# Attention in a hybrid decoder layer: bias rows broadcast by TensorE out of SBUF, and part of the last head pair's weights transposed by TensorE

## Chip, cores and metric

The kernel runs on one core of a Trainium2 chip. The metric is the device time of one execution in microseconds (us), taken as the median of several runs. The five engines of the core that matter here are TensorE (PE, with its weight loads shown apart as PEld), VectorE (DVE), ScalarE (ACT), GpSimd (POOL) and SyncE (SP), whose queue issues most of the DMAs.

## What is computed

One layer of a decoder with two parallel head groups, over 2048 tokens of width 1024. The part that the change touches is the attention group with forget gates: 8 heads of width 64, causal, with a logit bias that is a running sum of log forget gates.

```python
def fox_attention(q, k, v, f_pre):
    log_f = jax.nn.log_sigmoid(f_pre.astype(jnp.float32))
    c = jnp.cumsum(log_f, axis=1).transpose(0, 2, 1)
    ...
        s = jnp.einsum('bhqd,bhkd->bhqk', qi, kh).astype(jnp.float32) * scale
        s = s + ci[..., :, None] - c[:, :, None, :]
        s = jnp.where(kpos[None, :] <= qpos[:, None], s, -jnp.inf)
        pr = jax.nn.softmax(s, axis=-1).astype(vh.dtype)
        return jnp.einsum('bhqk,bhkd->bhqd', pr, vh)
```

The query's own `ci` is the same for a whole row and drops out of the softmax, so the kernel only needs `c` of the keys: one row of 2048 numbers per head, the same for all 128 queries of a block. Around it stand an input projection, a chunkwise mLSTM group, an output projection, a squared-ReLU MLP, a gated embedding and three norms.

## The kernel before, in words

**Stages.** The mLSTM group comes first (up to about 540 us), then the attention, then output projection, MLP, gate and final norm. Attention works on four pairs of heads, j = 0 to 3 (`fox_attn`, called in a loop over `NP`), and inside a pair on two heads, `hh`. While a pair is attended to, a *filler* supplies TensorE with other work: the projections of the next pair (`fox_z`, tiles zfq, zv, zfk) and the embedding (`ple_parts`, tile pp), or, in the last pair, half of the output projection (`wo_parts`, tile om, line 641).

**A head.** The 16 blocks of 128 queries are taken in nine steps (`ROWS`): block 15 alone, then the pairs (14, 0), (13, 1) up to (8, 6), then block 7 alone. A step has 16 blocks of 128x128 weights (the last has 8), held in two *units* of 8 blocks. For each step `fox_rows` does:

- lines 798 to 803: score matmuls into PSUM tiles s (a pool of `SB` = 3) in chunks of up to 512 keys;
- line 806: DVE adds the bias row and takes the running maximum, into an SBUF tile sp;
- line 821: ACT takes the exponential, with the maximum as its bias;
- lines 826 and 828: ACT casts a unit to f16 (tile ph, `PHB` = 4 buffers), and POOL or DVE writes the rest as a second f16 part beside it;
- line 830: one DMA transpose on SP's queue turns the unit's 16 blocks (8 high, 8 low) into tile pt (`PTB` = 3 buffers).

`fox_av` (lines 846 to 849) multiplies a step's transposed weights by the values. It runs `LAG` = 3 steps behind the scores: a finished step goes into `avq`, and `drain` takes out the oldest.

**The bias.** In the gates stage `cf`, the running sums of all heads, is transposed on TensorE into `crs` [128 x 128], one row for each head and key block (line 376). Line 379 writes it to DRAM as `crow`. At the start of each head, lines 890 to 893 fetch it in two halves (`sg` = 1, then 0) of 1024 keys: SP's queue issues a DMA that reads 8 rows of `crow` into all 128 partitions (512 KB), and DVE multiplies the tile by the score scale. `bias` has two buffers, so that a half can only be fetched when the head before has added that half for the last time, and the first step of a head needs half 0 first.

**What sets the order.** The program is written in this order, and a scheduler then gives each engine a fixed sequence of instructions; an engine works through its own in order, and a queue of SP issues in order.

## Time and profile before

| | us |
|---|---|
| median of 3 runs (2952.34 to 2958.37) | 2958.08 |
| the profiled execution | 2954.44 |
| its span in the trace | 2952.7 |
| PE busy (share of the span) | 2698.4 (91%) |
| DVE busy | 1621.7 (55%) |
| ACT busy | 1008.3 (34%) |
| POOL busy | 698.7 (24%) |

The profile is of one execution, so its terms are set against its own time of 2954.44 us, of which 2952.7 us are the span. Busy time is the union of an engine's instructions. The shares are means over stages of different kinds: in the MLP, which is more than half of the span, PE is busy nearly without a break.

### The profile page before, as it was taken

How to read it: one execution, taken by the hardware profiler on the slowest of the kernel's cores; microseconds unless marked ns; L12 is line 12 of the kernel's file. 1: busy time of each engine (PE TensorE's matmuls, PEld its weight loads, DVE VectorE, ACT ScalarE, POOL GpSimd, SP SyncE). 2: the span in 40 equal slices, each digit the busy share in tenths (PEclk: the TensorE clock that was granted, in tenths of full speed). 3: DMA queues.
4: the chain of work that ended last, by engine and by line, in shares of the span. 5: the costliest groups of instructions: out<-in, count | busy, mean ns of one | idle time of the engine just before them, and what ended most of it. 6: DMA issues, size and time to landing. Idle time of an engine off the chain costs nothing. (4 is left out here: it accounts for less than half of the span.)

```text
span 2952.7 us, 45034 instructions
## 1 busy us (share of the span) xinstructions
PE 2698.4 (91%) x18229; PEld 1507.1 (51%) x18229; DVE 1621.7 (55%) x3633; ACT 1008.3 (34%) x1686; POOL 698.7 (24%) x435
## 2 busy tenths in 40 slices
PE   4998999888878788788999999999999999999997
PEld 2756767555454554343344444444444444444686
DVE  6464654766757657556654444444444444445636
ACT  6244444465555555553411111111111111113532
POOL 1011110244343444343122111111212111111132
PEclk9999999989899989999999999999999999999999
DMA  9212220387686879996700000000000000002623
GB/s 243 45 44 59 58 47 20 94 167 137 139 166 133 165 169 219 196 205 222 148 29 29 29 29 16 28 15 29 29 29 29 29 29 16 28 15 43 143 69 136
DMA packets 535265, 256.36 MB, mean 87 GB/s; under 512 B 432784, under 2 KB 502672, under 8 KB 535056
## 3 DMA queue, kind: packets, MB, share of 16 engines
q1 hardware_dynamic: 525296, 236.66, 35.0%
q10 hardware_dynamic: 9760, 16.82, 1.8%
q8 instruction: 142, 2.33, 0.3%
q14 instruction: 67, 0.55, 0.1%
HBM read 113.88 MB, written 32.60 MB: 50 GB/s over the span
## 5 line engine op out<-in xcount | busy, mean ns | idle before, releaser
L1054 PE MATMUL d<-wd_hl,hid 128*128 128x512 f16 x3072 | 678.2, 380 | 8.4 <-DVE x L1059 8.2
L1036 PE MATMUL h<-y1t,wu_hl 128*128 128x512 f16 x3072 | 673.5, 379 | 0.5 <-issue 0.5
L1054 PEld LDWEIGHTS <-hid 128*128 128x128 f16 x3072 | 301.3, 98 | 375.0 <-issue 15.8
L1036 PEld LDWEIGHTS <-wu_hl 128*128 128x128 f16 x3072 | 300.5, 98 | 363.2 <-ACT y1y L200 1.0
L1059 DVE SCALAR_TENSOR_TENSOR x<-d,fac,x 128x512 f32<-128x512 f32 x512 | 373.8, 747 | 132.2 <-PE d L1054 131.8
L1044 POOL TENSOR_TENSOR hid<-r,hid 128x512 f16<-128x512 f32 x128 | 174.5, 1364 | 765.2 <-ACT hid L1043 659.1
L1042 DVE SCALAR_TENSOR_TENSOR r<-h,r 128x512 f32<-128x512 f32 x128 | 88.3, 690 | 458.2 <-ACT r L1040 458.1
L1040 ACT ACTIVATE r<-h 128x512 f32<-128x512 f32 x128 | 75.9, 594 | 766.8 <-PE h L1036 763.3
L828 POOL TENSOR_TENSOR ph<-sp,ph 128x1024 f16<-128x1024 f32 x119 | 255.9, 2164 | 283.3 <-ACT ph L826 219.3
L271 PEld LDWEIGHTS <-yt 128*128 128x128 f16 x3072 | 251.6, 101 | 40.1 <-issue 13.7
L260 PE MATMUL zqk<-yt,wqk_hl 128*128 128x512 f16 x768 | 188.7, 393 | 27.9 <-DMA yt<-yy 27.9
L821 ACT ACTIVATE sp<-sp,nb,fs 128x1024 f32<-128x1024 f32 (+3 forms) x192 | 177.9, 982 | 85.2 <-DVE nb L818 60.5
L798 PE MATMUL s<-K,Q 128*128 128x512 f16 (+3 forms) x320 | 117.9, 369 | 79.4 <-DVE mx L806 76.4
L846 PE MATMUL av<-vt,pt 128*128 128x65 f16 x1088 | 121.9, 199 | 67.3 <-DMA pt<-ph 55.6
L271 PE MATMUL zvo<-wvo_hl,yt 128*128 128x256 f16 x1536 | 175.0, 275 | 4.1 <-ACT wvo_hl L155 2.8
L1007 PE MATMUL pg<-wpg_hl,y2t 128*128 128x256 f16 x1536 | 171.0, 275 | 4.7 <-DVE x L1059 4.0
L1007 PEld LDWEIGHTS <-y2t 128*128 128x128 f16 x1536 | 151.6, 99 | 24.1 <-issue 5.1
L826 ACT CAST ph<-sp 128x1024 f16<-128x1024 f32 x136 | 137.8, 1038 | 67.9 <-DMA pt<-ph 62.6
L846 PEld LDWEIGHTS <-pt 128*128 128x128 f16 x1088 | 105.3, 100 | 75.1 <-DMA pt<-ph 67.8
L806 DVE CUSTOM_DVE_ANT_0 sp<-s,bias,mx 128x512 f32<-128x512 f32 (+2 forms) x192 | 124.5, 648 | 29.4 <-POOL ph L828 14.2
L260 PEld LDWEIGHTS <-wqk_hl 128*128 128x128 f16 x768 | 77.4, 101 | 105.5 <-ACT wqk_hl L155 25.9
L641 PEld LDWEIGHTS <-mix 128*128 128x128 f16 x768 | 76.4, 102 | 101.6 <-issue 27.7
(380 smaller groups left out, 3648.2 us busy)
## 6 DMA issues: line engine op xcount, KB each, us to landing
x<-in_x_dram SPq DMA_DIRECT2D x32, 512.0 KB, 5.8
wu_st<-in_w_up_dram SPq DMA_DIRECT2D x16, 1024.0 KB
wd_st<-in_w_down_dram SPq DMA_DIRECT2D x16, 1024.0 KB, 4.9
bias<-crow SPq DMA_DIRECT2D x16, 512.0 KB, 5.9
pled<-fox_st ACTq DMA_DIRECT2D x32, 256.0 KB, 2.8
wod<-spare ACTq DMA_DIRECT2D x32, 256.0 KB, 5.0
wos<-wod SPq DMA_DIRECT2D x32, 256.0 KB, 3.9
emb<-pled SPq DMA_DIRECT2D x32, 256.0 KB, 3.0
```

What stands on the lines that cost most here:

```text
L260: PE.matmul(ps, lhsT=hl[:, a, kt, m * P:(m + 1) * P], rhs=yT[g][b][:, kt, :], start=i == 0, stop=i == 3 * KT - 1)
L271: PE.matmul(ps[:, 0:n], lhsT=yT[g][b][:, kt, o:o + P], rhs=hl[:, a, kt, 0:n], start=i == 0, stop=i == 3 * KT - 1)
L806: V.tensor_tensor_reduce(out=st[u][:, o * P:(o + n) * P], in0=ps[:, 0:n * P], in1=bias[kb // 8][:, kb % 8 * P:(kb % 8 + n) * P], scale=1.0 ...
L821: A.activation(sl_, sl_, AF.Exp, bias=nb, scale=fs[:, 0:1])
L826: A.copy(ph[:, 0:1024], st[u])
L828: eng.tensor_sub(ph[:, 1024:2048], st[u], ph[:, 0:1024])
L846: PE.matmul(ar, lhsT=pt[:, o, :], rhs=vs[:, 0:65], start=kb == 0, stop=False)
L1007: PE.matmul(ps, lhsT=aT[t // 4][ya][:, kt, o:o + P], rhs=hl[:, wa, kt, :], start=i == 0, stop=i == 3 * KT - 1)
L1036: PE.matmul(ps, lhsT=wu[:, a, kt, m * P:(m + 1) * P], rhs=y1T[g][b][:, kt, :], start=i == 0, stop=i == 3 * KT - 1)
L1044: T.tensor_sub(hid[:, 1, m], r2, hid[:, 0, m])
L1054: PE.matmul(ps, lhsT=hid[:, a, m, t * P:(t + 1) * P], rhs=wd[:, b, m, hf * 512:(hf + 1) * 512], start=i == 0, stop=i == 5)
L1059: V.scalar_tensor_tensor(xs, ps, fac, xs, ALU.mult, ALU.add)
```

## The change

It has two parts.

The first takes the bias broadcast off the DMA. `crs` becomes a constant tile that stays in SBUF, and `crow` and its DMA are gone. For each half of 1024 keys there are now two PSUM tiles of the score pool (`cb`, tag "s"). Each is filled by four f32 matmuls, whose stationary operand is one column of the identity repeated 128 times and whose moving operand is `crs`; each writes one row of `crs` to all 128 partitions. ACT then copies the tile to SBUF with the score scale as its factor, which replaces DVE's multiplication.

The second part concerns the last head pair alone (h of 6 and 7). Of the two units of a step, the second is no longer transposed by DMA: `fox_rows` puts it into `turns`, and `turn` transposes it when `drain` comes to it (one step ahead of its use): 16 transposing matmuls of 128x128 f16 into two PSUM tiles of the pool that the filler uses (tag "z"), and two ACT copies to pt. There are 8 such units in each of the two heads.

```diff
-    crow = dr.tile([P, P], F32, name="crow")
+    crs = const.tile([P, P], F32, name="crs")
+    identh = const.tile([P, P], F16, name="identh")
+    V.tensor_copy(identh, ident)
...
-        crs = gp.tile([P, P], F32, name="crs")
         V.tensor_copy(crs, tps[:, 0:P])
-        SP.dma_start(out=crow, in_=crs)
...
-            SP.dma_start_transpose(out=pt, in_=ph)
+            if h >= FH - 2 and u == 1:
+                turns[tag] = pt, ph
+            else:
+                SP.dma_start_transpose(out=pt, in_=ph)
             pts.append(pt)
         return pts
+
+    turns = {}
+
+    def turn(e):
+
+        tag = f"{e[3]}_{e[4][0]}" if e[0] else None
+        if tag not in turns:
+            return
+        pt, ph = turns.pop(tag)
+        for a in range(2):
+            ps = psz.tile([P, GT], F32, tag="z", name=f"pt{tag}_{a}").bitcast(F16)
+            for b in range(8):
+                bs = slice(b * P, (b + 1) * P)
+                PE.transpose(out=ps[:, bs], in_=ph[:, a * 1024 + b * P:a * 1024 + b * P + P],
+                             identity=identh)
+            A.copy(pt[:, 8 * a:8 * a + 8].rearrange("p b s -> p (b s)"), ps)
...
             e = avq.pop(0)
+            turn(e)
+            if avq:
+                turn(avq[0])
...
-                SP.dma_start(out=b.rearrange("p (t s) -> p t s", s=P),
-                             in_=crow[h * NT + 8 * sg:h * NT + 8 * sg + 8, :]
-                             .partition_broadcast(P))
-                V.tensor_scalar(b, b, fs[:, 2:3], None, op0=ALU.mult)
+                for q in range(2):
+                    ps = fpp.tile([P, 512], F32, tag="s", name=f"cb{h}_{sg}_{q}", bufs=SB)
+                    for t in range(4):
+                        r = h * NT + 8 * sg + 4 * q + t
+                        PE.matmul(ps[:, t * P:(t + 1) * P],
+                                  lhsT=ident[:, r:r + 1].to_broadcast([P, P]), rhs=crs,
+                                  start=True, stop=True)
+                    A.activation(b[:, q * GT:(q + 1) * GT], ps, AF.Copy, scale=fs[:, 2:3])
                 bias[sg] = b
```

The scheduler lays out the new instructions anew. The first place is PE where the third head (names with a 2) ends and the fourth (names with a 3) begins. s2_7_0_4 is the last score chunk of the old head, s3_15 the first step of the new one, s3_14 its second; pt2_10 to pt2_7 are the transposed weights of the old head's last four steps. One matmul of a group stands for all of it. Before:

```order
L803 MATMUL s2_7_0_4_9601<-fneg_87,identb_85 128x128
...
L798 MATMUL s3_15_0_0_9675<-K_5163,Q1_5944 128x512
...
L846 MATMUL av_6239<-vt1_5945,pt2_10_1_9043 128x65
...
L846 MATMUL av_6239<-vt1_5945,pt2_9_0_9244 128x65
...
L846 MATMUL av_6239<-vt1_5945,pt2_8_0_9426 128x65
...
L846 MATMUL av_6239<-vt1_5945,pt2_7_0_9613 128x65
...
L798 MATMUL s3_15_0_12_9690<-K_5163,Q1_5944 128x512
...
L798 MATMUL s3_14_0_0_9860<-K_5163,Q1_5944 128x512
```

and now:

```order
L803 MATMUL s2_7_0_4_9662<-fneg_87,identb_85 128x128
...
L916 MATMUL cb3_1_0_9729<-crs_382,ident_75 128x128 x4
...
L865 MATMUL av_6260<-vt1_5946,pt2_10_1_9104 128x65
...
L916 MATMUL cb3_0_1_9748<-crs_382,ident_75 128x128 x4
...
L798 MATMUL s3_15_0_0_9756<-K_5164,Q1_5945 128x512
...
L798 MATMUL s3_15_0_12_9771<-K_5164,Q1_5945 128x512
...
L865 MATMUL av_6260<-vt1_5946,pt2_9_0_9305 128x65
...
L798 MATMUL s3_14_0_0_9941<-K_5164,Q1_5945 128x512
...
L865 MATMUL av_6260<-vt1_5946,pt2_8_0_9487 128x65
```

Before, all four waiting steps of the old head are multiplied out ahead of the new head's fourth chunk. Now one of them is, and after it each step of the old head stands behind a step of scores of the new one, as inside a head.

The second place is ACT at the same boundary. ph2_7_0 is the cast of the old head's last unit, sp3_15_0 the first exponential of the new head. Before:

```order
L826 CAST ph2_8_1_9428<-sp2_8_1_9388 128x1024
L821 ACTIVATE sp2_7_0_9595<-sp2_7_0_9595,nb2_7_0_9607,fs1_6476 128x1024
L613 ACTIVATE fox_st_5119<-pp8_0_9789,pe8_9333 128x512
L826 CAST ph2_7_0_9610<-sp2_7_0_9595 128x1024
...
L821 ACTIVATE sp3_15_0_9673<-sp3_15_0_9673,nb3_15_0_9696,fs1_6476 128x1024
```

and now:

```order
L826 CAST ph2_8_1_9489<-sp2_8_1_9449 128x1024
L821 ACTIVATE sp2_7_0_9656<-sp2_7_0_9656,nb2_7_0_9668,fs1_6497 128x1024
L919 ACTIVATE bias3_1_9728<-cb3_1_0_9729,fs1_6497 128x512
L826 CAST ph2_7_0_9671<-sp2_7_0_9656 128x1024
L919 ACTIVATE bias3_1_9728<-cb3_1_1_9735,fs1_6497 128x512
L919 ACTIVATE bias3_0_9741<-cb3_0_0_9742,fs1_6497 128x512
L919 ACTIVATE bias3_0_9741<-cb3_0_1_9748,fs1_6497 128x512
```

Three of the four new copies, both halves of the bias that the first step needs among them, stand behind the cast of the old head's last unit.

The third place is the last head (names with a 7), first SP's queue near its end. Before:

```order
L830 DMA_TRANSPOSE pt7_11_0_15244<-ph7_11_0_15241 128x16x128
L830 DMA_TRANSPOSE pt7_11_1_15249<-ph7_11_1_15246 128x16x128
L830 DMA_TRANSPOSE pt7_10_0_15355<-ph7_10_0_15352 128x16x128
L830 DMA_TRANSPOSE pt7_10_1_15360<-ph7_10_1_15357 128x16x128
L830 DMA_TRANSPOSE pt7_9_0_15481<-ph7_9_0_15478 128x16x128
```

and now:

```order
L833 DMA_TRANSPOSE pt7_11_0_15593<-ph7_11_0_15590 128x16x128
L833 DMA_TRANSPOSE pt7_10_0_15723<-ph7_10_0_15720 128x16x128
L833 DMA_TRANSPOSE pt7_9_0_15868<-ph7_9_0_15865 128x16x128
```

and, on ACT, where the copies of step 11's second unit came in:

```order
L652 ACTIVATE spare_13709<-om1_10_16019,invo1_1_13754 128x512
L851 COPY pt7_11_1_15598<-pt7_11_0_15954 128x1024
L851 COPY pt7_11_1_15598<-pt7_11_1_15964 128x1024
L826 CAST ph7_8_1_16015<-sp7_8_1_15975 128x1024
```

Every second transpose is gone from the queue, and two copies stand on ACT among the casts of the step that is three later.

## Rows read from the trace of the kernel before

**Rows 1.** The page: busy time, and PE, clock and DMA in 40 slices.
```profile
PE 2698.4 (91%) x18229; PEld 1507.1 (51%) x18229; DVE 1621.7 (55%) x3633; ACT 1008.3 (34%) x1686; POOL 698.7 (24%) x435
...
PE   4998999888878788788999999999999999999997
...
PEclk9999999989899989999999999999999999999999
DMA  9212220387686879996700000000000000002623
```
**Rows 2.** Busy time by stretch: all the attention, and its last head pair.
```profile
564.00:1322.00 758.00, 606.46 (x6315) 369.29 (x6316) 486.01 (x1510) 413.35 (x528) 307.52 (x158) 0.92 0.81 164
1138.90:1322.00 183.10, 145.44 (x1323) 77.67 (x1324) 105.03 (x334) 100.00 (x116) 81.86 (x41) 0.92 0.92 199
```
**Rows 3.** Timeline of DVE across the boundary of heads three and four (start, duration).
```profile
833.49 0.75 DVE L806 CUSTOM_DVE_ANT_0 sp<-s,bias,mx 128x512 f32<-128x512 f32 x1
...
841.26 0.75 DVE L893 TENSOR_SCALAR bias<-bias,fs 128x1024 f32<-128x1024 f32 x1 [3.78 <-DMA bias<-crow]
...
857.30 0.75 DVE L893 TENSOR_SCALAR bias<-bias,fs 128x1024 f32<-128x1024 f32 x1 [1.30 <-DMA bias<-crow]
858.20 0.69 DVE L806 CUSTOM_DVE_ANT_0 sp<-s,bias 128x512 f32<-128x512 f32 x1
```
**Rows 4.** Timeline of SP's queue across the same boundary.
```profile
836.28 1.00 SPq L890 DMA_DIRECT2D bias<-crow  x1
837.44 14.37 SPq L830 DMA_TRANSPOSE pt<-ph  x4
851.87 0.68 SPq L890 DMA_DIRECT2D bias<-crow  x1
```
**Rows 5.** Timeline of ACT across the same boundary: the old head's last cast.
```profile
838.87 1.03 ACT L826 CAST ph<-sp 128x1024 f16<-128x1024 f32 x1
```
**Rows 6.** Busy time by stretch, last cast to next head's first add (columns PE, PEld, DVE, ...).
```profile
core 0: us, PE busy (x) PEld busy (x) DVE busy (x) ACT busy (x) POOL busy (x), PEclk, DMA share, GB/s
649.40:654.50 5.10, 2.81 (x48) 2.53 (x46) 2.57 (x4) 0.79 (x3) 5.10 (x4) 1.00 1.00 240
...
839.90:858.20 18.30, 9.59 (x164) 9.17 (x162) 4.36 (x11) 1.79 (x6) 0.66 (x1) 0.81 1.12 191
...
1115.10:1138.90 23.80, 16.31 (x166) 9.52 (x163) 14.82 (x42) 3.77 (x7) 3.54 (x3) 0.86 1.13 223
...
sum 104.10, PE 71.35 PEld 46.27 DVE 54.78 ACT 15.81 POOL 20.80; mean PE 10.19 PEld 6.61 DVE 7.83 ACT 2.26 POOL 2.97
```
**Rows 7.** Busy time by stretch inside the heads: the fourth head, and the sum of all.
```profile
858.20:921.40 63.20, 53.94 (x568) 32.60 (x566) 42.45 (x141) 42.92 (x55) 30.09 (x14) 1.00 0.70 132
...
sum 613.10, PE 506.06 PEld 303.08 DVE 414.85 ACT 363.99 POOL 263.58; mean PE 56.23 PEld 33.68 DVE 46.09 ACT 40.44 POOL 29.29
```
**Rows 8.** Timeline of PE in the mLSTM stage: f32 matmuls in a row.
```profile
187.53 0.39 PE L508 MATMUL i<-cst,qk 128*128 128x129 f32 x2
187.76 0.27 PE L519 MATMUL k<-ident,qk 128*128 128x128 f32 x1
187.87 0.59 PE L260 MATMUL zqk<-yt,wqk_hl 128*128 128x512 f16 x2
```
**Rows 9.** Groups by line in the attention (busy, mean ns of one, idle before).
```profile
L826 ACT CAST ph<-sp 128x1024 f16<-128x1024 f32 x136 | 137.8, 1038 | 67.9 <-DMA pt<-ph 62.6 <-DMA mixd<-po 5.0
...
L652 ACT ACTIVATE spare<-om,invo 128x512 f32<-128x512 f32 x32 | 21.4, 683 | 48.1 <-PE om L641 38.3 <-PE av L849 6.2 <-DMA wod<-spare 1.9
...
L893 DVE TENSOR_SCALAR bias<-bias,fs 128x1024 f32<-128x1024 f32 x16 | 13.4, 840 | 32.5 <-DMA bias<-crow 32.5
```
**Rows 10.** Timeline of PE: f16 matmuls of 128 columns in a row.
```profile
839.37 1.61 PE L271 MATMUL zv<-fox_hl,yt 128*128 128x128 f16 x26
```
**Rows 11.** Who waited for whom, 1120 to 1322 us (total, times, longest).
```profile
PE av L846 <- DMA pt<-ph: 29.4, 18, 4.4
```

## The prediction

> **What bounds the kernel now.** I began with the page. PE is busy for 91% of the span, but not evenly: in the slices of the attention, the 8th to the 18th, its digit is 7 or 8, the DMA digit mostly 6 to 9, and the clock's digit falls to 8 in places, while after them PE stays at 9 almost to the end [rows 1]. What the change can win lies in those slices. The table by stretch sizes it: of the 758.0 us from the first score to the last weighted sum PE is busy for 606.5, at a mean granted clock of 0.92 (of its two levels, 1.2 and 2.4 GHz, it is at the lower for some of the time), and the DMA engines for 0.81 [rows 2]. Some 150 us of PE's time are idle there.
>
> Next I looked for where. At the end of the third head DVE adds the last bias at 833.5; then it has no score to add until 858.2, and it stands ready at 841 and at 857 for a bias half [rows 3]. SP's queue shows why: the half that the next head needs first is issued at 851.9, behind four transposes that take 14.4 us to issue [rows 4]. So the fetch is not slow in itself; it is queued behind the very transposes that the old head's end leaves over. There are seven such boundaries between eight heads.
>
> Not all of such a gap can close. ACT casts the old head's last unit until 839.9 [rows 5], and the new bias copies stand behind that cast in ACT's order. So for each boundary I took the stretch from the end of that cast to the new head's first add: they run from 5.1 us to 23.8, 104.1 in all [rows 6]. In them PE is busy for 71.4 us, idle for 32.7.
>
> **The boundaries, part by part.** The DMA fetches go (16, two a head), and so do 16 multiplications on DVE of 13.4 us in all [rows 9]. DVE is busy for 486 of the 758 us [rows 2], so I count nothing for those; should DVE be late somewhere, 13 us is the most they can give.
>
> In their place comes a chain: four groups of matmuls, four copies, the first score chunk, the first add. A copy of 128x512 from PSUM takes 0.68 us (the om tile) [rows 9]. Three of them behind the cast are 2.0 us, and the slots that they free for the scores, the score matmuls and the hand-overs are some 2 us more, an estimate: 4 us a boundary, 28 for seven. The scores start 104 - 28 = 76 us earlier, summed over the boundaries.
>
> How much of that reaches the end? At least PE's own idle time in the part of the stretches that closes: 32.7 x 76 / 104 = 24 us. At most all 76. The difference is work that PE now does in the gap (old heads' weighted sums, filler) and must then do inside the heads. There PE is busy for 506 of 613 us, and for 53.9 of 63.2 in the fourth head [rows 7]. That is no wide margin, so I take a value nearer to the lower end, 24 plus a third of the way, **40 us**. What makes up the third is that the idle time before a clock dip is gone with the gap (0.81 in one of the stretches [rows 6]), and that PE's order now puts a step of new scores between the old head's weighted sums, so that they wait less for their transposes.
>
> The broadcast matmuls are new on PE: 16 halves of 8, so 128 f32 matmuls. The trace shows an f32 matmul of 129 columns and two passes starting at 187.53 and the next instruction at 187.76 [rows 8]: 0.23 us, 29 us for all. They stand just where the score chain waits for ACT, beside old work; hidden wholly they cost 0, in full 29. I take half, **15 us**. Their PSUM slots come from the score pool of three, so a score chunk behind them waits for a copy; that is in the 4 us. ACT's 32 copies, 22 us, are in the chain where they matter, and beside it ACT is busy for 413 of 758 us [rows 2]. SP's queue loses 16 issues, and the transposes behind them start that much earlier; I leave this in the third. Boundaries: **-25 us**.
>
> **The last pair.** 16 units (eight in each of two heads) leave the DMA queue for PE and ACT. On PE that is 256 transposes of 128 columns. The nearest row for f16 at this width gives 26 matmuls in 1.61 us, 62 ns each [rows 10], hence 16 us; that is the value I take. The nearest row for a transpose, an f32 one, lasts 0.27 us, though the next matmul starts 0.11 us after it [rows 8]; by its whole duration the sum is 70 us, which I keep as the upper end.
>
> The Trainium skill speaks against this part: TensorE: Matmul & The Clock Gate, Part 4: PE-mode transpose, puts a 128x128 transpose at some 275 ns in the context of a kernel. By that the 256 would cost 70 us where I count 16. The duration in the trace agrees with the figure, the distance to the next start does not.
>
> On ACT it is 32 copies of 128x1024. A cast of that size takes 1.04 us out of SBUF, and two copies of half the size out of PSUM 1.37 [rows 9]: 33 to 44 us. The pair's 183 us have 100 of ACT busy [rows 2], so there is room; what hides them is that `turn` runs one step ahead of use. If that cover is gone, PE stands at the weighted sum for a copy: that is the slow case below. For the gain: in the last two heads' stretch PE waits for transposes for 29.4 us in 18 places [rows 11], with the DMA engines at 0.92 [rows 2]. Halving the transposes should take away about half, 15 us. The end of the pair hangs on the transposes alone; with one of two off the queue I take 5 us there, an estimate. Together 16 - 15 - 5 = **-4 us**, with ends of +70 (all waits staying) and -20.
>
> **The sum.** 2954.4 - 25 - 4 = 2925 us, against the profiled execution's own time. The median of the runs lies 3.6 us above that execution and the lowest 2.1 below; I make no allowance for it.
>
> **The rivals.**
>
> *The heads take it all.* If the steps inside a head wait mostly for each other (score, add, exponential, cast, transpose) and not for PE, all 76 us arrive, the broadcasts hide, and the last pair gives 10: 2954 - 86 = 2868. For it: PE has 107 us of idle time inside the heads [rows 7]. Against it: the fourth head, with PE busy for 85%, is already near what PE can do.
>
> *PE gets nothing back.* Work moves out of the gaps into heads that are full, the broadcasts are paid in full: -24 + 29 - 4, so 2955, no change. For it: PE is busy for 69% of those 104 us [rows 6], hardly less than in the heads, so the gaps are idle for DVE and ACT far more than for PE. Against it: the fetch's delay is real, and PE's idle 33 us are there to be had.
>
> *The turned units hold up the last pair.* This is the slow side. PE goes through its order, and a turned unit puts transposes, two ACT copies and the weighted sum in a row; ACT's copies stand among casts that wait for buffers and exponentials that wait for DVE. If a unit takes the transposes at their whole duration, 16 x 0.27 = 4.4 us, and PE then stands for one copy of 1.2, it costs 5.6 us; 16 units are 90, and with the 20 given back 70. Less the boundaries' 25 the kernel is at 2999. It decides from (25 + 20) / 16 = 2.8 us a unit on. For it: rows 8 and the full ACT queue. Against it: 16 f16 matmuls of that width take 1.0 us by rows 10, and the units are turned a step early.
>
> That the broadcast does not close the gap at all, since its copies wait behind the old head's cast, is counted in the 104 us already.
>
> **How the numbers follow.** The forecast has 0.55; its bounds are a gain of 24 to 60 for the boundaries, a cost of 0 to 29 for the broadcasts, and -20 to +10 for the last pair; as these will not all stand at one end together, I give it 2895 to 2948. The heads taking it all has 0.20, PE getting nothing back 0.14, the slow last pair 0.11. A range from 2868 to 2960 leaves out half of the second and nearly all of the last, 2 in 10. A measurement of this kernel can tell 0.2%, 5.9 us, from no change. Faster by more than that: nearly all of the forecast (0.53), all of the second (0.20) and a little of the third (0.03), 0.76. Within it: most of the third, 0.12. Slower: the last and the rest, 0.12.
>
> **What would show it.** Right: DVE's wait for the bias fetch is gone, a head's first add follows the old head's last cast by some 4 us instead of 5 to 24, PE is busy for a larger share of a shorter attention (some 730 us instead of 758), and the old head's weighted sums lie between the new head's scores. In the last pair PE's wait for transposes halves, and no wait of PE for the new copies takes its place. Wrong: the gaps close but the steps inside the heads grow longer by as much (PE's bound), or waits of the weighted sums for ACT's copies stand in the last pair (the slow case), or the broadcasts start late because a score slot is not free.

## The result and the profile after

The changed kernel takes 2986.05 us (median of 6 runs, 2982.36 to 2991.31) where the kernel before takes 2955.21 (6 runs on the same chip): a ratio of 1.0114, with a 95% interval of 1.0100 to 1.0128. It is slower by some 34 us (31 by the medians). The forecast was 2925, with a range of 2868 to 2960. In what follows, microseconds against the kernel before are a run's ratio less one, times 2950.

The page of the profiled execution (2987.12 us, span 2985.0), the lines that answer to [rows 1]:

```profile
PE 2734.1 (92%) x18741; PEld 1551.2 (52%) x18741; DVE 1615.9 (54%) x3618; ACT 1056.0 (35%) x1750; POOL 698.6 (23%) x435
...
PE   4988999978788787888899999999999999999997
...
PEclk9999999999899898999999999999999999999999
DMA  9212220376676787566710000000000000001623
```

PE has 36 us more to do, and the digits of the attention's slices are still 7 and 8. The table by stretch of the changed kernel shows all the attention (first add to last weighted sum) and the last pair (from the end of the pair before):

```profile
567.00:1349.40 782.40, 639.96 (x6797) 410.17 (x6795) 476.59 (x1497) 458.19 (x587) 307.14 (x158) 0.92 0.68 141
1157.20:1349.40 192.20, 156.56 (x1594) 95.52 (x1591) 99.20 (x313) 127.03 (x149) 79.81 (x40) 0.91 0.59 140
```

The attention is 24 us longer than in [rows 2], at the same mean clock, with PE busy for 33 us more and the DMA engines relieved (0.68 after 0.81). Behind it another 5 us are lost; the start comes 3 us later. The second row of [rows 2] starts later than the second row here; cut as here, the last pair took 187.5 us before.

Did the gaps close? Yes, and nearly as forecast. DVE at the boundary of heads three and four, then ACT:

```profile
842.10 0.75 DVE L806 CUSTOM_DVE_ANT_0 sp<-s,bias,mx 128x512 f32<-128x512 f32 x1 [0.35 <-PE s L803]
...
851.36 0.68 DVE L806 CUSTOM_DVE_ANT_0 sp<-s,bias 128x512 f32<-128x512 f32 x1
```

```profile
847.45 1.04 ACT L826 CAST ph<-sp 128x1024 f16<-128x1024 f32 x1
848.38 1.83 ACT L919 ACTIVATE bias<-cb,fs 128x512 f32<-128x512 f32 x3
```

Between the last add of the old head and the first of the new one there are now 9 us where there were 25 [rows 3]; the wait for the fetch is gone, and the new head's first add comes 2.9 us behind the old head's last cast. But the time came back inside the heads. To see it, I cut the attention into two kinds of stretch for both kernels: from the old head's last cast to the new head's first add (seven), and from a head's first add to its last cast (eight; the sum in [rows 7] ends a head at its last add and counts the tail, so its idle time is another). For the kernel before the first sum is in [rows 6] (104.10, PE busy 71.35); the second, its table by stretch, is

```profile
sum 635.20, PE 520.81 PEld 314.88 DVE 421.44 ACT 394.17 POOL 281.44; mean PE 65.10 PEld 39.36 DVE 52.68 ACT 49.27 POOL 35.18
```

and for the changed kernel the seven and the eight are

```profile
sum 35.90, PE 25.48 PEld 19.67 DVE 17.89 ACT 18.68 POOL 18.48; mean PE 3.64 PEld 2.81 DVE 2.56 ACT 2.67 POOL 2.64
...
sum 721.60, PE 594.64 PEld 377.77 DVE 446.88 ACT 429.62 POOL 283.46; mean PE 74.33 PEld 47.22 DVE 55.86 ACT 53.70 POOL 35.43
```

The boundaries are 68 us shorter and the heads 86 us longer (the tail behind the last cast gives the other 6). PE's idle time is what matters: 32.7 us of it stood in the boundaries and 10.4 stand there now, while in the heads it rose from 114.4 to 127.0.

What the new instructions took, groups by line of the changed kernel (busy, mean ns of one, idle before; an f32 matmul has two records):

```profile
L916 PE MATMUL cb<-crs,ident 128*128 128x128 f32 x255 | 38.6, 306 | 7.5 <-ACT bias L919 7.5
...
L851 ACT COPY pt<-pt 128x1024 f16<-128x1024 f16 x32 | 30.6, 1008 | 6.6 <-PE av L868 6.6
...
L849 PE MATMUL pt<-identh,ph 128*128 128x128 f16 x256 | 20.9, 231 | 18.2 <-ACT spare L652 6.3 <-ACT ph L826 6.1 <-ACT pt L851 3.0
L919 ACT ACTIVATE bias<-cb,fs 128x512 f32<-128x512 f32 x32 | 20.5, 685 | 4.5 <-PE cb L916 4.4
```

And for what PE waited in the attention, before and then after:

```profile
PE s L798 <- DVE mx L806: 76.4, 43, 4.9
PE av L846 <- DMA pt<-ph: 55.6, 35, 6.6
```

```profile
PE s L798 <- DVE mx L806: 89.2, 42, 6.2
PE av L865 <- DMA pt<-ph: 10.5, 7, 3.2
```

The waits for transposes fell by 45 us and the waits of scores for a free slot rose by 13; 18 us stand in front of the new transposes and 7.5 in front of the broadcasts. In the last pair none of PE's listed waits is for a DMA transpose any more; before, these were 28.1 us.

### The profile page after: what moved, and what is told of

Its sections match the earlier page's. It is cut to its first block, busy times and chain, and to the rows that moved or that the text cites. A ratio compares the mean times of both kernels' runs of the same rounds, so it can differ in the third digit from the quotient of the medians.

```text
span 2985.0 us, 46039 instructions
## 1 busy us (share of the span) xinstructions
PE 2734.1 (92%) x18741; PEld 1551.2 (52%) x18741; DVE 1615.9 (54%) x3618; ACT 1056.0 (35%) x1750; POOL 698.6 (23%) x435
## 5 line engine op out<-in xcount | busy, mean ns | idle before, releaser
L271 PEld LDWEIGHTS <-yt 128*128 128x128 f16 x3072 | 245.0, 100 | 38.4 <-issue 14.7
L260 PE MATMUL zqk<-yt,wqk_hl 128*128 128x512 f16 x768 | 188.1, 392 | 28.1 <-DMA yt<-yy 28.1
L866 PE MATMUL av<-vt,pt 128*128 128x64 f16 x1088 | 121.0, 200 | 0.0
```

The costliest lines, as they stand in the source:

```text
L260: PE.matmul(ps, lhsT=hl[:, a, kt, m * P:(m + 1) * P], rhs=yT[g][b][:, kt, :], start=i == 0, stop=i == 3 * KT - 1)
L271: PE.matmul(ps[:, 0:n], lhsT=yT[g][b][:, kt, o:o + P], rhs=hl[:, a, kt, 0:n], start=i == 0, stop=i == 3 * KT - 1)
```

## The experiments

The theories. **T1**: closing the gap gives PE little back, since its idle time only moves into the heads, and the broadcasts are paid in full (the second rival of the prediction). **T2**: the new order of PE's program costs, not the broadcasts. **T3**: closing the gap is worth what the forecast says, and the turned units lose more than that.

One reading limit first: the kernels with the whole first part differ from each other only in the last pair, and yet their first three pairs took from 583.8 to 591.2 us in the profiled executions. A difference below some 7 us in a single stretch is not read. By the intervals given, a difference between two runs that are each set against the kernel before is uncertain by some 5 us. Diffs are against the changed kernel where nothing else is said.

**The two parts apart.** The first part alone:

```diff
-            if h >= FH - 2 and u == 1:
+            if False and u == 1:
```

> The change's first part alone: the bias rows are broadcast by TensorE, and all weights are turned by the DMA queue as before. T1 (the broadcasts are paid in full, because closing the gap at a head's start only moves TensorE's idle time into the steps behind it): the loss of the first three pairs stays, 20 to 27 us over the kernel before. T3 (closing the gap gives back 25 to 40 us, and the turned units lose more than that): 5 to 25 us faster than before. Both would read the first three pairs in the trace: T1 has their end 20 to 25 us later than before, T3 earlier.

Measured: 1.0029 (1.0018 to 1.0039), +9 us. Between the two theories: a loss, but a small one. In the trace the first three pairs end at 1150.2 where they ended at 1134.5, 16 us later: T3 had them earlier, T1 20 to 25 later. The last pair then takes 174.7 us where it took 187.5, so part of the delay comes back there; where the pairs meet, the new head is further on than before, so the cut is not quite the same. Its seven boundaries and eight heads:

```profile
sum 32.60, PE 23.42 PEld 17.39 DVE 19.13 ACT 16.21 POOL 18.59; mean PE 3.35 PEld 2.48 DVE 2.73 ACT 2.32 POOL 2.66
...
sum 705.30, PE 584.05 PEld 367.05 DVE 449.46 ACT 408.36 POOL 283.78; mean PE 73.01 PEld 45.88 DVE 56.18 ACT 51.04 POOL 35.47
```

71.5 us went out of the boundaries and 70.1 came into the heads, almost one for one. PE's idle time fell by 23.5 us in the boundaries and rose by 7 in the heads. Its busy time fell by 48 us in the boundaries and rose by 63 in the heads. That is moved work and broadcasts: of the 224 records of broadcasts from the first add on, 167 stand in the last 8 us before an old head's last cast, so inside the heads by this cut.

The second part alone (the fetch by DMA as before, the turns as changed):

```diff
-                for q in range(2):
...
+                SP.dma_start(out=b.rearrange("p (t s) -> p t s", s=P),
+                             in_=crow[h * NT + 8 * sg:h * NT + 8 * sg + 8, :]
+                             .partition_broadcast(P))
+                V.tensor_scalar(b, b, fs[:, 2:3], None, op0=ALU.mult)
```

> The change's second part alone: every second unit of the last pair is turned by TensorE, and the bias rows come by DMA as before. T1: the last pair's waits for turned weights (29 us) go and its transposes cost 16 to 18 us, and what is left idle moves: within 6 us of the kernel before. T3: 40 us or more slower than before. A third reading, that the turns are a gain spoilt by the bias broadcasts, would have it 10 us or more faster than before.

Measured: 1.0059 (1.0044 to 1.0074), +17 us, between the figures of T1 and T3, and no gain for the third reading. The two parts alone add to +26, both together are +34. So most of the loss is the turned units': 17 alone, 25 on top of the first part.

**The broadcasts' price.** Each matmul issued twice (diffs in this group against the first part alone):

```diff
-                        PE.matmul(ps[:, t * P:(t + 1) * P],
-                                  lhsT=ident[:, r:r + 1].to_broadcast([P, P]), rhs=crs,
-                                  start=True, stop=True)
+                        for a in range(2):
+                            PE.matmul(ps[:, t * P:(t + 1) * P],
+                                      lhsT=ident[:, r:r + 1].to_broadcast([P, P]), rhs=crs,
+                                      start=True, stop=True)
```

> The first part alone with each of the 128 broadcast matmuls issued twice (the second writes the same values again), so TensorE does some 31 us more and everything else is as in the first part alone. T1 (TensorE paces the heads, so its time is paid in full): 25 to 31 us slower than the first part alone. T2 (the loss comes from the new order of the scores, adds and weighted sums at the heads' starts, and the broadcasts themselves fit into idle time): within 8 us of the first part alone.

Measured: 1.0110 (1.0094 to 1.0126), +32 us, 24 more than the first part alone (20 by the medians). The distances from each broadcast matmul's start to the next matmul's (each counted as 0.5 us at most), summed over the attention from the first add on, are 33 us in the first part alone and 60 here: 27 us of PE cost 20 to 24, short of the 25 to 31 of T1. T2, by which the broadcasts themselves cost nothing, falls. But the order did not stay as expected: PE's sequence, the broadcasts set aside, differs from that of the first part alone from the first head on, so a share of the 24 for moved filler is not excluded.

A quarter of them:

```diff
+                        if t == 0:
                             PE.matmul(ps[:, t * P:(t + 1) * P],
...
-                    A.activation(b[:, q * GT:(q + 1) * GT], ps, AF.Copy, scale=fs[:, 2:3])
+                    A.activation(b[:, q * GT:(q + 1) * GT].rearrange("p (t s) -> p t s", s=P),
+                                 ps[:, 0:P].unsqueeze(1).to_broadcast([P, 4, P]), AF.Copy,
+                                 scale=fs[:, 2:3])
```

> The first part alone with 32 broadcast matmuls instead of 128: of four rows one is broadcast and used four times, so the bias is not the reference's. TensorE does some 23 us less than in the first part alone, and the order stays. Doubling the broadcasts cost 20 us for some 31 us of TensorE. If that price holds downwards (the broadcasts are paid at about two thirds, and closing the gap gives something back, about 11 us): 13 to 17 us faster than the first part alone, so 4 to 8 us faster than before. If closing the gap gives nothing (T1): not faster than before, within 5 us of it. If the gap is worth the 40 us of the forecast: 20 us or more faster than before.

Measured: 0.9958 (0.9942 to 0.9973), 12 us faster than before and 21 faster than the first part alone, for 23 us less of PE (33 to 10). That is more than the 13 to 17 expected. Here too filler moved from the first head on, and the order did not stay the same.

The same price with the whole bias, each row kept as a high and a low f16 row in one tile, so that one f16 matmul with two ones in its column adds them:

```diff
-    crs = const.tile([P, P], F32, name="crs")
+    crs = const.tile([P, 2, P], F16, name="crs")
+    sel = const.tile([P, 64], F16, name="sel")
+    V.tensor_add(sel, ident[:, 0:64], ident[:, 64:128])
...
-        PE.transpose(out=tps[:, 0:P], in_=cf.rearrange("p n t -> p (n t)"), identity=ident)
-        V.tensor_copy(crs, tps[:, 0:P])
+        cf2 = gp.tile([P, 256], F32, name="cf2")
+        for g in range(4):
+            V.tensor_copy(cf2[:, g * 64:g * 64 + 64],
+                          cf.rearrange("p n t -> p (n t)")[:, g // 2 * 64:g // 2 * 64 + 64])
+        for g in range(2):
+            PE.transpose(out=tps[:, g * P:(g + 1) * P], in_=cf2[:, g * P:(g + 1) * P],
+                         identity=ident)
+        ct = tps[:, 0:2 * P].rearrange("p (g s) -> p g s", s=P)
+        V.tensor_copy(crs, ct)
+        V.tensor_sub(crs[64:128], ct[64:128], crs[64:128])
...
-                                  lhsT=ident[:, r:r + 1].to_broadcast([P, P]), rhs=crs,
+                                  lhsT=sel[:, r % 64:r % 64 + 1].to_broadcast([P, P]),
+                                  rhs=crs[:, r // 64],
```

> The first part alone with the broadcasts made cheap and the bias whole: each row is kept as two f16 rows (the high part and the rest) in one tile, so that one f16 matmul of 128 columns with a selector of two ones broadcasts their sum, instead of one f32 matmul; the weights are turned by the DMA queue as before. TensorE does some 23 us less than in the first part alone, as with 32 broadcasts instead of 128. If what that run showed was the price of TensorE's time: 9 to 14 us faster than before. If it gained from the wrong bias or by an order of its own: within 5 us of before.

Measured: 0.9985 (0.9973 to 0.9998), 4 us faster than before and 13 faster than the first part alone, for 24 us less of PE (33 to 9). That is under the 9 to 14 expected for the price of PE's time and inside the expectation's second reading, by which the run before gained in part by an order of its own, or by the rows that it leaves out; which of the two was not tested. The whole interval of this version still lies below both kernels, though barely below the kernel before. Boundaries and heads:

```profile
sum 27.80, PE 20.08 PEld 11.65 DVE 14.06 ACT 15.59 POOL 16.84; mean PE 2.87 PEld 1.66 DVE 2.01 ACT 2.23 POOL 2.41
...
sum 699.90, PE 569.69 PEld 352.37 DVE 460.11 ACT 408.71 POOL 287.09; mean PE 71.21 PEld 44.05 DVE 57.51 ACT 51.09 POOL 35.89
```

Here the broadcasts are nearly gone from PE's work, the boundaries are 76 us shorter, just what the prediction took, and the heads 65 longer. PE's idle time: 25 us less in the boundaries, 16 more in the heads.

From the three runs the gap can be priced. With 10 us of broadcasts left the gain is 12, at the price of that run (21 for 23) without any 21; with 9 left it is 4, at the price of that run (13 for 24) without any 9. So **closing the gap is worth 9 to 21 us**, and the broadcasts cost 18 to 30, which is more than that. This is an estimate: it takes the price to be in proportion to the matmuls' time, each end carries its runs' 5 us, and the three orders differ.

**The fetch in another queue,** against the kernel before:

```diff
-                SP.dma_start(out=b.rearrange("p (t s) -> p t s", s=P),
+                A.dma_start(out=b.rearrange("p (t s) -> p t s", s=P),
```

> The kernel before with one line changed: the bias fetch is issued from ScalarE's queue, so that it does not stand behind the transposes on SyncE's queue. TensorE does nothing more than before, the gap at a head's start should get shorter by the fetch's wait. T1 (idle time only moves): within 6 us of the kernel before though the gap closes. T3, and the forecast's own term (closing the gap is worth 40 us): 20 to 40 us faster than before. If the gap does not close, the run tells nothing.

Measured: 1.0108 (1.0089 to 1.0128), +32 us, a miss for both. The boundaries shrank only from 104 to 82 us, and something new was lost: from the transposes' line, before and then here, who waited for it (us, times) and the time from issue to landing.

```profile
  PE av L846: 55.6, 35
...
DMA to landing us min/median/max: 4.3/5.2/10.1
```

```profile
  PE av L846: 87.9, 35
...
DMA to landing us min/median/max: 4.3/4.9/15.5
```

The weighted sums wait 32 us longer for transposes, of which single ones now land after 15.5 us. The fetch of 512 KB then runs beside them and no longer between them. That this overlap is the whole loss isn't shown; as a test of the gap the run tells little.

**Why the turned units lose.** Half of ACT's copies left out:

```diff
-            A.copy(pt[:, 8 * a:8 * a + 8].rearrange("p b s -> p (b s)"), ps)
+            if a == 0:
+                A.copy(pt[:, 0:8].rearrange("p b s -> p (b s)"), ps)
...
+                lo = 0 if h >= FH - 2 and (at + kb) // 8 == 1 else 8
-                PE.matmul(ar, lhsT=pt[:, 8 + o, :], rhs=vs[:, 0:65], start=False, stop=kb == i)
+                PE.matmul(ar, lhsT=pt[:, lo + o, :], rhs=vs[:, 0:65], start=False, stop=kb == i)
```

> The changed kernel with half of ScalarE's copies of turned weights left out: only the high half of a turned unit is copied, and the weighted sums use it in place of the low half too; TensorE's transposes are all there. The 16 copies left out took 1.0 us each, 16 us. Theory A (the turned units cost through ScalarE, whose copies come between the exponentials and casts of the last pair): 8 to 14 us faster than the changed kernel, so 17 to 26 us slower than before. Theory P (they cost through TensorE, which waits in front of the transposes and does them): within 5 us of the changed kernel, about 31 us slower than before.

Measured: 1.0100 (1.0084 to 1.0116), +29 us, 4 better than the changed kernel. Theory A falls.

Half of PE's transposes left out:

```diff
-        for a in range(2):
-            ps = psz.tile([P, GT], F32, tag="z", name=f"pt{tag}_{a}").bitcast(F16)
-            for b in range(8):
...
+        ps = psz.tile([P, GT], F32, tag="z", name=f"pt{tag}_0").bitcast(F16)
+        for b in range(8):
+            bs = slice(b * P, (b + 1) * P)
+            PE.transpose(out=ps[:, bs], in_=ph[:, b * P:b * P + P], identity=identh)
+        for a in range(2):
```

> The changed kernel with half of TensorE's transposes of turned weights left out: only the high half is turned, and it is copied twice, so ScalarE's copies are all there; one slot of PSUM is taken per unit instead of two. The 128 transposes left out take some 8 us of TensorE, and the waits in front of the second half go with them (18 us of idle stand in front of all 256). Theory P: 8 to 14 us faster than the changed kernel. Theory A: within 5 us of it.

Measured: 1.0060 (1.0046 to 1.0074), +18 us, 16 better than the changed kernel, nearly twice the 9 us of the transposes left out. Theory P, at first sight.

The copies on DVE:

```diff
-            A.copy(pt[:, 8 * a:8 * a + 8].rearrange("p b s -> p (b s)"), ps)
+            V.tensor_copy(pt[:, 8 * a:8 * a + 8].rearrange("p b s -> p (b s)"), ps)
```

> The changed kernel with the 32 copies of turned weights on VectorE instead of ScalarE. VectorE is busy for 99 of the last pair's 192 us, ScalarE for 127. Theory A: 8 to 20 us faster than the changed kernel, unless VectorE's adds are then late in the same way. Theory P: within 5 us of the changed kernel, since TensorE waits for a copy either way.

Measured: 1.0123 (1.0108 to 1.0139), +36 us, level with the changed kernel, as theory P has it. ACT's load was not the price.

Half of the transposes, but both slots:

```diff
-            for b in range(8):
+            for b in range(4):
...
-                PE.transpose(out=ps[:, bs], in_=ph[:, a * 1024 + b * P:a * 1024 + b * P + P],
+                PE.transpose(out=ps[:, bs], in_=ph[:, a * 512 + b * P:a * 512 + b * P + P],
...
-            A.copy(pt[:, 8 * a:8 * a + 8].rearrange("p b s -> p (b s)"), ps)
+            A.copy(pt[:, 8 * a:8 * a + 8].rearrange("p (c b) s -> p c (b s)", c=2),
+                   ps[:, 0:512].unsqueeze(1).to_broadcast([P, 2, 512]))
```

> The changed kernel with half of the transposes left out and both slots of PSUM kept: each of a unit's two slots takes four transposes and is copied twice over (so the low half and half of the high half of the turned weights are missing), ScalarE's copies are all there. If the turned units cost through TensorE's transposing itself and the half less of it made the run with half the transposes faster: level with that run, about 18 us slower than before. If they cost through the PSUM slots that the output projection also takes: level with the changed kernel, 30 to 36 us slower than before.

Measured: 1.0102 (1.0081 to 1.0122), +30 us: 4 better than the changed kernel, with the same number of transposes that gave 16 in one slot. By the expectation this speaks for the slots. In the traces of the last pair PE is busy for 151.2 us here and for 145.7 with one slot, at granted clocks of 0.89 and 0.92, and idle for 41.5 and 33.1; 6.1 us of waits in front of the transposes for slots that ACT frees stand here alone. So less transposing by itself does not give the loss back.

Another place in the order:

```diff
             turn(e)
-            if avq:
-                turn(avq[0])
             if e[0]:
                 fox_av(*e[1:])
             else:
                 posts.append([PD_, *e[1:]])
+            if avq:
+                turn(avq[0])
```

> The changed kernel with a step's transposes on TensorE placed behind the weighted sums of the step before instead of ahead of them; no work more or less. If the turned units cost by waits (TensorE stands in front of the transposes for a cast or a slot, with weighted sums that are ready behind them): 6 to 15 us faster than the changed kernel, so 19 to 28 us slower than before. If they cost by the work of the transposes, or the wait comes back as one for the copies: within 5 us of the changed kernel.

Measured: 1.0110 (1.0088 to 1.0132), +32 us, no change, so the reading by weighted sums that stand behind falls. In its trace PE still waits for 11 us in front of the transposes and for 6 for the copies.

That left the waits and slots around a turn, without the work. The queue turns everything, and at the places of the turns stand two small matmuls a unit (32 in all, not the 64 that I wrote into the expectation) with copies of 16 columns, first behind the unit's casts, then, as a change to that, on a constant:

```diff
-            else:
-                SP.dma_start_transpose(out=pt, in_=ph)
+            SP.dma_start_transpose(out=pt, in_=ph)
...
+            PE.transpose(out=ps[:, 0:P], in_=ph[:, a * 1024:a * 1024 + P], identity=identh)
-            A.copy(pt[:, 8 * a:8 * a + 8].rearrange("p b s -> p (b s)"), ps)
+            A.copy(scr[:, 16 * a:16 * a + 16], ps[:, 0:16])
```

> The first part alone, all weights turned by the DMA queue, and at the places of the turned units two small matmuls on TensorE (one block of the high and one of the low half turned, 64 of them in the last pair, some 4 us), each into a PSUM slot of the output projection's ring, with a copy of 16 columns that frees it. Nobody uses them. They wait for the unit's casts and for a slot. If the turned units cost by what TensorE waits for in front of them: 10 to 20 us slower than the first part alone, so 19 to 29 us slower than before. If they cost by the transposes' and copies' own time: within 6 us of the first part alone, 3 to 15 us slower than before.

```diff
-            PE.transpose(out=ps[:, 0:P], in_=ph[:, a * 1024:a * 1024 + P], identity=identh)
+            PE.transpose(out=ps[:, 0:P], in_=identh, identity=identh)
```

> The same, but the two small matmuls turn a constant, so they wait for a PSUM slot alone and not for a cast. If the slots of the output projection's ring are the price: level with the run that also waits for the casts, 10 us or more slower than the first part alone. If the wait for the casts is: within 5 us of the first part alone.

Measured: both 1.0088 (1.0070 to 1.0105 and to 1.0106), +26 us, 17 more than the first part alone. So the wait for the casts is not what these two lose by. The same without a slot (this and the next two against the run on a constant):

```diff
-            ps = psz.tile([P, GT], F32, tag="z", name=f"pt{tag}_{a}").bitcast(F16)
-            PE.transpose(out=ps[:, 0:P], in_=identh, identity=identh)
+            ps = avt[0][:, a, 0, 96:128]
+            PE.matmul(ps, lhsT=identh, rhs=identh[:, 0:32], start=True, stop=True)
```

> The run with the two small matmuls on a constant, with their results put into unused columns of the weighted sums' PSUM bank instead of into slots of the output projection's ring; the copies of 16 columns stay. If the slots are the price: within 5 us of the first part alone, 4 to 14 us slower than before. If added instructions on TensorE and ScalarE at these places are, whatever they write: level with that run, some 26 us slower than before. A wait for the bank, which the weighted sums share, would also read as a loss, and then the run tells nothing.

Measured: 1.0084 (1.0066 to 1.0102), +25 us, level with the run on slots. A wait for the shared bank is possible here (ACT waits for 15 us for these matmuls in its trace, 2.6 in the run on slots), so the slots are not cleared: this run speaks for added instructions whatever they write, the one with half the transposes in two slots spoke for slots. Last, the matmuls without the copies, and the copies without the matmuls:

```diff
-            A.copy(scr[:, 16 * a:16 * a + 16], ps[:, 0:16])
```

> The run with two small matmuls on a constant per turned unit, without the copies: TensorE writes into a slot of the output projection's ring and nobody reads it, so ScalarE waits for nothing. If ScalarE's copy, which stands in ScalarE's order and waits for TensorE to reach the place, is the price: within 5 us of the first part alone, 4 to 14 us slower than before. If TensorE's side or the order is: 20 to 30 us slower than before.

```diff
-            ps = psz.tile([P, GT], F32, tag="z", name=f"pt{tag}_{a}").bitcast(F16)
-            PE.transpose(out=ps[:, 0:P], in_=identh, identity=identh)
-            A.copy(scr[:, 16 * a:16 * a + 16], ps[:, 0:16])
+            A.copy(scr[:, 16 * a:16 * a + 16], identh[:, 0:16])
```

> The same without the matmuls: ScalarE copies 16 columns of a constant twice per turned unit, and nothing waits for TensorE. TensorE's order is that of the first part alone, word for word. If ScalarE's added instructions by themselves are the price: 20 to 30 us slower than before. If the wait for TensorE, TensorE's side or the order is: within 5 us of the first part alone, 4 to 14 us slower than before.

Measured: 1.0067 (1.0052 to 1.0082), +20, and 1.0046 (1.0028 to 1.0064), +14 us: 11 and 5 more than the first part alone. Both lie at the edge of the reading "TensorE's side or the order"; the 5 us are not clear of noise, since the intervals of this run and of the first part alone overlap. The 32 matmuls for 11 us would be 0.34 us each, over five times the 62 ns of [rows 10].

But the traces do not show that price where the matmuls stand. Up to the last pair PE's order is the same in all these runs as in the first part alone, so they can be compared from there on (us in the profiled executions):

| | last pair | behind the attention |
|---|---|---|
| the first part alone | 174.7 | 1629.8 |
| small matmuls behind the casts | 181.8 | 1640.6 |
| on a constant | 177.7 | 1639.4 |
| on a constant, without a slot | 182.5 | 1638.1 |
| without the copies | 175.5 | 1635.0 |
| copies alone | 171.9 | 1632.6 |
| the changed kernel | 192.2 | 1635.6 |

The last pair of the run without the copies by stretch, and the longest waits of PE in it:

```profile
1158.40:1333.90 175.50, 142.19 (x1370) 82.09 (x1367) 100.16 (x308) 97.60 (x117) 79.76 (x40) 0.91 0.89 193
```

```profile
PE av L861 <- DMA pt<-ph: 18.3, 9, 8.2
PE s L799 <- DVE mx L807: 14.6, 10, 4.3
```

Its pair is 0.8 us longer than that of the first part alone, and no wait in front of the small matmuls is listed; most of what it and the run on a constant lose lies behind the attention. Behind it, PE's matmuls come in the order of the first part alone again in both. The six kernels without instructions for turned units take 1627 to 1631 us there, the twelve with them 1633 to 1641. Why is not known, and a single difference of this size is near the reading limit.

The real turns do show in the pair: it is 17.5 us longer, of which PE is busy for 14.8. So the work of the turns and their waits account for the pair, and what an instruction at these places costs by itself is not shown. What PE loses by moved filler (its order inside the pair differs in all these runs but the copies alone) stays open too, and so does the difference of 12 us between one slot and two.

## Why the prediction was wrong

*The gap.* Right: the fetch's wait is gone, boundaries of 104 us became 36 (28 in the split version, with 4 us each as forecast), 68 to 76 us. The first failed step is "How much of that reaches the end?". I took 40 us and gave 24 as the least, PE's idle time in the part that closes. The runs show 9 to 21. The step held that idle time which closes is gained. It closed (32.7 us to 7.7 in the split version), but PE's idle time inside the heads grew by 16 us. In the attention of the split version PE's longest waits are still these two, 76.4 and 55.6 us before:

```profile
PE s L806 <- DVE mx L814: 81.1, 54, 10.6
PE av L873 <- DMA pt<-ph: 40.4, 25, 6.0
```

Of the two things that were to make up the third above 24, the waits for transposes did get shorter (55.6 to 40.4), but the waits of the scores for a free slot did not; and the mean granted clock hardly moved (0.92 before, 0.93 in the split version). That those waits hold the heads is argued from the numbers and not shown by a run. The sum over both kinds of stretch is the measure: 147.1 us idle before, 137.9 in the split version.

*The broadcasts.* A matmul took what it was forecast to (eight started from 845.14 to 847.00, 0.23 us each). "I take half, 15 us" was mis-sized: doubling and quartering price them at nine tenths, the split version at half; 18 to 30 us. Three quarters of them stand in the last 8 us before the old head's last cast. In the seven stretches of 8 us PE was busy for 38.0 of 56 us before and is for 41.8 with the first part alone, so there was idle time beside them; why so little of it hid them is not shown.

*The last pair.* The second failed step, and here the sign failed: forecast -4, measured +17 alone and +25 on top of the first part. The work was right: the 256 transposes go by in 17 us from start to start (each counted as 0.5 us at most), 67 ns each. The Trainium skill (TensorE: Matmul & The Clock Gate, Part 4: PE-mode transpose) puts one at some 275 ns, by which an estimate for all is 70 us. A record here lasts 231 ns, not far from that, but the records overlap, and the starts decide. The waits for DMA transposes fell by more than the half that I counted. The cover of the copies that I named, "`turn` runs one step ahead of use", held: PE waits for them for 2.2 us at the weighted sums and for 3.0 us for slots. What I put at nothing was PE's waiting in front of the transposes themselves, for casts and slots: 18.2 us, as much as the relieved queue gave back. And the tail got longer, not shorter (18.7 us from the last cast before, 20.6 with the first part alone, 24.9 with the turns), where I had counted -5. The last pair by stretch with the first part alone, to be set against the second row of the changed kernel's table above:

```profile
1150.20:1324.90 174.70, 141.72 (x1336) 79.83 (x1333) 98.73 (x307) 97.06 (x116) 79.44 (x40) 0.92 0.88 193
```

With the turns the pair takes 17.5 us more, PE is busy for 15 us more, and the DMA engines are at 0.59 where they were at 0.88. The relieved queue had held PE up for 17.3 us there (its waits for transposes in the run without turns). So the pair is accounted for: 17 us of work, 17 given back, 18 of new waits. It is 17.5 of the 25; 6 more stand behind the attention, and their cause stays open. Why the new waits cost what they do stays open too: with half of ACT's copies and with the turns moved in the order they fell to 10 and 11 us, but the pair only to 189.0 and 189.7.

*The rivals.* "The heads take it all" falls with the first part alone at +9 us. "PE gets nothing back" was nearest to the first part (2955, but with the turns as a gain). "The turned units hold up the last pair" had the place right and the mechanism wrong: PE stands for ACT's copies for 5.2 us in all, and the transposes do not cost their whole duration. Measured are 25 / 16 = 1.6 us a unit, below its 2.8; the slow side was reached because the boundaries gave nothing to set against it. The range ended at 2960, too low for that.

## What to carry to other kernels

A gap on one engine is worth what the bounding engine idles over the whole stretch, not in the gap: sum its idle time before and after across both, since what closes at one place can open at the next. Work put onto the busiest engine to close it should be counted in full until a run shows cover; the same broadcast at a quarter of the matmul time turned +9 us into -4. When work moves from a queue to the bounding engine, ask what the engine will wait for in front of it: here 18 us of new waits took the place of 17 old ones, and the work came on top. And a loss should be looked for by stretches before it is given a mechanism: the run with 32 small matmuls lost 11 us, of which the pair that they stand in shows 0.8.

## What the runs showed that I had not expected

With the fetches of 512 KB moved off the queue of the transposes onto another, the kernel was 32 us slower; the longest transpose landed after 15.5 us where it had been 10.1, and the median landing was no longer (4.9 us after 5.2). And the runs with small matmuls in the last pair took 5 to 11 us longer behind the attention in the profiled executions, where PE's order was the same in all but one of them.
